# Attention queries and keys projected with tokens as columns, values for all heads at once, row sums of squares gathered through DRAM

## The chip, the core and the metric

The kernel runs on one core of one Trainium2 chip. The metric is the device time of one execution in microseconds, lower is better. The names of the profile are used throughout: PE is TensorE (matmuls), PEld its weight loads, DVE is VectorE, ACT is ScalarE, POOL is GpSimd, SP is SyncE, whose queue issues most DMAs. A bank is one 128 x 512 float32 tile of the accumulator memory that PE writes.

## What is computed

One decoder layer on 1024 tokens of width 1024, in float32: a normalised input goes through one input projection; half of its columns feed four heads of differential attention (this case), the other half a gated delta rule that runs chunk by chunk over the sequence (called the scan below); both go through one output projection and a squared-ReLU MLP. The part that the change touches:

```python
da_q = rms_norm(da_q.reshape(B, S, DA_HEADS, 2, DA_QK_DIM), q_norm_w[l])   # 4 heads x 2 maps x 64
da_k = rms_norm(da_k.reshape(B, S, DA_HEADS, 2, DA_QK_DIM), k_norm_w[l])
da_v = da_v.reshape(B, S, DA_HEADS, DA_V_DIM)                              # 4 heads x 128
...
s = jnp.einsum('bqhcd,bkhcd->bhcqk', qb, k) * scale       # causal, two maps per head
p = jax.nn.softmax(s, axis=-1)
a = p[:, :, 0] - lam * p[:, :, 1]
out = jnp.einsum('bhqk,bkhe->bqhe', a, v)
```

So each query and each key is divided by the root of the mean square of its own 64 numbers, and multiplied by a learned weight, before the products.

## The kernel before, in words

Every large product is made of three float32r matmuls (high part by high part, high by low, low by high), so a 128-deep slice of a product costs three matmuls. `hH` and `hL` hold the normalised input as high and low parts, features on partitions, tokens as columns.

The program has four stretches on PE. First the input norm, the z gate and the scan's own projections (`ps_z`, `ps_dn`; the latter, in `trn`, already has weights stationary and 512 tokens moving). Second the attention projections (`ps_qk`), with the scan (`ps_A`, `ps_o` of lines 1079 and 1095) and the attention of heads 0 and 1 (`ps_sc` scores, `ps_at` transposes of the exponentials, `ps_o` of line 1465) put between. Third the output projection (`ps_op`) with the attention of heads 2 and 3 between. Last the MLP (`X`, `Y`, `Z`).

From the second stretch on, the order of all engines is written by a planner, the class `Interleave`. Streams of PE work with priorities (the scan first, then attention, then `da_units`, then the output projection) yield small pieces; tasks stand for the work of ACT, DVE, POOL and SP, with assumed costs (`act`, `vec`, `powr`, `load`, `STORE`). The planner keeps its own clock and emits each engine's instructions in the order in which its model would start them. On the chip each engine then runs its own list in that order, and waits where an operand is not there.

`da_units` (line 1196) is the filler of the second stretch. It makes 48 units: for each of two head groups `g` the keys, the queries and the values, each for 8 blocks of 128 tokens. A unit has 24 matmuls into 256 columns of a bank: 128 tokens stationary (`hH`, `hL`), 256 weight columns moving. Two banks (`pj`) take turns. `normed` (line 1218) then empties a unit: for values ACT copies it and POOL stores it; for queries and keys ACT squares it (line 1235) and copies it (line 1238), DVE sums the squares (`sn`, line 1241), DVE and POOL make the inverse root (`rn`, lines 938 and 940), and DVE multiplies (line 1247). `da_turns` (line 1157) turns the result by two PE transposes (`ps_qkt`, lines 1163 and 1164) so that features come on partitions, ACT applies the learned weight (line 1172), and POOL stores it to `q_d` or `k_d`.

`head_loads` (line 1279) later loads a head's keys and splits them in high and low parts (`KS`), then loads its values (`vt`); `query_loads` loads a block of queries. `open_unit` in `scores` makes the scores of one block of 128 queries; for each map one DVE instruction adds the mask and finds the row maximum (line 1349), ACT takes the exponential with that maximum as bias (line 1342), `joined` combines the two maps, and `values` multiplies with `vt`.

Weights come in pieces of 128 x 512 through two buffers (`wraw`), are split by ACT (line 979) and DVE (line 981), and lie in two sets of buffers that take turns (`wH`, `wL`), so the weights of the next unit but one can be split only when a set is free.

Of the kernel before, what the change touches and what calls it, by code (L numbers as in the profile page):

```python
# [9 lines left out]
F32 = mybir.dt.float32  # L10
# [22 lines left out]
INVERSES = 500.0  # L33
# [16 lines left out]
class Interleave:  # L50
# [101 lines left out]

    def until(self, res):
        return self.held.get(self.first(res[0]) if isinstance(res, list) else res, 0.0)
# [46 lines left out]
def tile_hymba_layer(  # L201
    ctx: ExitStack,
    tc: tile.TileContext,
    x, x_cols, w1_cols, w_z, w_units, lambda_q1, lambda_k1, lambda_q2, lambda_k2, q_norm_w, k_norm_w,
# [50 lines left out]
    q_d = dram.tile([2, NT, P, 2 * P], F32, name="q_d")  # L255
    k_d = dram.tile([2, 2, P, SEQ], F32, name="k_d")
    v_d = dram.tile([2, 2, P, NT, P], F32, name="v_d")
# [425 lines left out]
    def dn_proj(kind):  # L683
        for pr in range(2):
            with tc.issue_after(x_last.ins) if kind == 1 and pr == 0 else ExitStack():
                w = load_unit(w_units[6 + 2 * kind + pr])
# [218 lines left out]
    ap = dctx.enter_context(tc.tile_pool(name="ap", bufs=1, **right))  # L905
    sdctx = ExitStack()
# [12 lines left out]
    def bank_tile(pool, res, name):  # L919
        return pool.tile([P, 512], F32, tag=f"{res[0]}{res[1]}", name=name)  # L920

    state = dict(scan=False, da=0, proj=False, attn=False, free=False, out=False, o1=0, o2=0, gates=0, begun=0, units=0,
                 turned=0, rows=0, started=0, popped=0, valued=0, first=False, op=0)
# [11 lines left out]
    def root(o, ss, scale, pool, tag, n):  # L935
        yield vec(n)
        t = pool.tile([P, n], F32, tag=tag, name=tag) if pool else laid(tag)
        V.tensor_scalar(t, ss, scale, EPS, ALU.mult, ALU.add)
        yield powr(n)
        G.tensor_tensor(o, t, neghalf[:, :n], ALU.pow)  # L940
# [206 lines left out]

    def x_loads():
        yield when(lambda: state["scan"])
        for tb in tiles:  # L1150
            yield load(5300.0)
            nc.sync.dma_start(accs[tb], x2[tb * P:(tb + 1) * P, :])
            yield flow.t + 6000.0

    late, accs, over = [], {}, set()

    def da_turns():
        for i in range(4 * NT):
            yield lambda: late[0][0].done if late and state["units"] >= 4 else None, None
            r = yield from flow.bank("px")  # L1160
            _, g, kind, tb, qn = late.pop(0)
            pt = bank_tile(px, r, "ps_qkt")
            T.transpose(pt[:, 0:P], qn[:, 0:P], ident)
            T.transpose(pt[:, P:2 * P], qn[:, P:2 * P], ident)
            flow.pe(2 * TR)
            state["rows"] -= 1

            def weighed(r=r, pt=pt, g=g, kind=kind, tb=tb):
                wv = qw if kind == 0 else kw
                yield "S", 370.0  # L1170
                qa = sd.tile([P, 256], F32, tag="qa", name="qa", bufs=4)
                S.activation(qa, pt[:, 0:256], AF.Copy, scale=wv)
                flow.leave(r)
                yield STORE
                if kind == 0:
                    nc.gpsimd.dma_start(q_d[g, tb], qa)
                else:
                    nc.gpsimd.dma_start(k_d[g, :, :, tb * P:(tb + 1) * P].rearrange("h p t -> p h t"),
                                        qa.rearrange("p (h t) -> p h t", h=2))
                yield None  # L1180
                state["turned"] += 1

            flow.task(1, weighed(), "sd")
# [7 lines left out]
    def group_done(g, last):  # L1191
        yield when(lambda: state["turned"] >= 2 * NT * (g + 1))
        yield last
        state["da"] = g + 1

    def da_units():
        n = 0
        for i, (g, kind) in enumerate(todo_da):
            job = jobs[i]
            state["begun"] = i  # L1200
            for j in range(NT):
                tb = NT - 1 - j if i == len(todo_da) - 1 else j
                sl = slice(tb * P, (tb + 1) * P)
# [1040 lines left out]
```

## Time and profile before

The profiled execution took 1221.5 us, of which the span (first to last instruction of the core) is 1219.7 us; the rest, 1.8 us, lies around it. Three runs without a profile took 1221.91 to 1222.18 us, median 1221.97, so the profiled execution stands 0.5 us below the median.

| | span | PE | DVE | ACT | POOL |
|---|---|---|---|---|---|
| busy us | 1219.7 | 1208.5 | 848.9 | 630.7 | 163.6 |
| instructions | | 6807 | 1642 | 1293 | 219 |

A busy PE is one that has some matmul under way; since matmuls overlap (each is shown for longer than the distance to the next one), the distance from start to start, seen in the timeline, tells what a matmul costs. The second stretch runs from 223.1 us (first `ps_qk`) to 452.7 us (first `ps_op`), the third to 601.7 us (first `X`).

### The profile page before, as it was taken

How to read it: one execution, taken by the hardware profiler on the slowest of the kernel's cores; microseconds unless marked ns; L12 is line 12 of the kernel's file. 1: busy time of each engine (PE TensorE's matmuls, PEld its weight loads, DVE VectorE, ACT ScalarE, POOL GpSimd, SP SyncE). 2: the span in 40 equal slices, each digit the busy share in tenths (PEclk: the TensorE clock that was granted, in tenths of full speed). 3: DMA queues.
4: the chain of work that ended last, by engine and by line, in shares of the span. 5: the costliest groups of instructions: out<-in, count | busy, mean ns of one | idle time of the engine just before them, and what ended most of it. 6: DMA issues, size and time to landing. Idle time of an engine off the chain costs nothing.

```text
span 1219.7 us, 18864 instructions
## 1 busy us (share of the span) xinstructions
PE 1208.5 (99%) x6807; PEld 1037.2 (85%) x6807; DVE 848.9 (70%) x1642; ACT 630.7 (52%) x1293; POOL 163.6 (13%) x219
## 2 busy tenths in 40 slices
PE   9999999999999999999999999999999999999998
PEld 8978888899999988888878888888888888888887
DVE  5879897646468876897797655566579754777543
ACT  6588643345356765586666544455554333333331
POOL 2423210044336331012100000000000000000000
PEclk9999999999999999999999999999999999999999
DMA  9334654445654564223438343453479555423301
GB/s 348 98 112 123 189 154 80 95 133 173 229 200 141 149 151 160 71 44 110 155 97 293 138 141 136 156 190 138 160 272 382 221 185 186 148 103 104 138 35 69
DMA packets 160837, 189.26 MB, mean 155 GB/s; under 512 B 61240, under 2 KB 116840, under 8 KB 160744
## 3 DMA queue, kind: packets, MB, share of 16 engines
q1 hardware_dynamic: 157144, 178.62, 45.0%
q0 software_dynamic: 3456, 9.44, 2.2%
q8 instruction: 53, 0.87, 0.3%
q14 instruction: 40, 0.33, 0.1%
q10 hardware_dynamic: 144, 0.00, 0.0%
HBM read 127.21 MB, written 60.82 MB: 154 GB/s over the span
## 4 chain that ended last, share of the span: by engine, by line
PE 92%; DVE 3%; ACT 1%; DMA 1%; issue 1%; SPq 0%; POOL 0%; POOLq 0%; ACTq 0%; DVEq 0%
PE X L1824 4%; PE X L1823 4%; PE X L1825 4%; PE X L2145 4%; PE X L2143 4%; PE X L2144 4%; PE ps_qk L1210 4%; PE ps_qk L1211 3%; PE ps_qk L1212 3%; PE ps_dn L279 3%; PE ps_dn L281 3%; PE ps_dn L280 3%; PE ps_o L1465 2%; PE ps_op L1609 2%; PE Y L1825 2%; PE ps_op L1611 2%
## 5 line engine op out<-in xcount | busy, mean ns | idle before, releaser
L1700 ACT CAST hH<-ur 128x1024 fp32r<-128x1024 f32 x56 | 58.9, 1051 | 173.3 <-PE Y L2144 89.8
L1701 DVE TENSOR_TENSOR hL<-ur,hH 128x1024 fp32r<-128x1024 f32 x56 | 68.4, 1223 | 80.7 <-ACT hH L1700 80.7
L1210 PE MATMUL ps_qk<-wH,hH 128*128 128x256 f32 x384 | 114.8, 299 | 1.2 <-DVE sn L1241 1.2
L1701 DVE TENSOR_TENSOR op<-raw,op 128x1024 fp32r<-128x1024 f32 x48 | 58.7, 1224 | 74.3 <-PE X L1824 40.4
L1211 PE MATMUL ps_qk<-wL,hH 128*128 128x256 f32 x384 | 108.8, 283 | 0.0
L1212 PE MATMUL ps_qk<-wH,hL 128*128 128x256 f32 x384 | 108.6, 283 | 0.0
L2143 PE MATMUL X<-hH 128*128 128x512 f32 x224 | 87.1, 389 | 0.0
L2144 PE MATMUL X<-hL,hH 128*128 128x512 f32 x224 | 87.1, 389 | 0.0
L2145 PE MATMUL X<-hH,hL 128*128 128x512 f32 x224 | 87.1, 389 | 0.0
L1210 PEld LDWEIGHTS ps_qk<-wH,hH 128*128 128x128 f32 x384 | 73.3, 191 | 4.0 <-DVE sn L1241 1.6
L279 PE MATMUL ps_dn<-hH,wH 128*128 128x512 f32 x192 | 76.0, 396 | 0.5 <-ACT cp L695 0.5
L280 PE MATMUL ps_dn<-hL,wH 128*128 128x512 f32 x192 | 75.5, 393 | 0.0
L281 PE MATMUL ps_dn<-hH,wL 128*128 128x512 f32 x192 | 75.3, 393 | 0.0
L1211 PEld LDWEIGHTS ps_qk<-wL,hH 128*128 128x128 f32 x384 | 73.4, 191 | 0.1
L1212 PEld LDWEIGHTS ps_qk<-wH,hL 128*128 128x128 f32 x384 | 73.2, 191 | 0.0
L1701 DVE TENSOR_TENSOR hL<-dw,hH 128x1024 fp32r<-128x1024 f32 x56 | 68.3, 1219 | 1.8 <-ACT hH L1700 1.6
L1700 ACT CAST op<-raw 128x1024 fp32r<-128x1024 f32 x48 | 50.5, 1052 | 34.8 <-PE Y L1825 19.9
L1700 ACT CAST hH<-dw 128x1024 fp32r<-128x1024 f32 x56 | 58.7, 1048 | 10.9 <-DMA dw<-in_w_down_dram 6.0
L699 DVE SCALAR_TENSOR_TENSOR cy<-cp,pv,cy 128x512 f32<-128x512 f32 x72 | 58.4, 813 | 5.9 <-ACT cy L697 5.0
L1342 ACT ACTIVATE pexp<-pexp,mx 128x128 f32<-128x128 f32 (+7 forms) x64 | 49.6, 776 | 10.3 <-DVE mx L1349 9.8
L1609 PE MATMUL ps_op<-wH,hH 128*128 128x512 f32 x128 | 54.4, 425 | 0.0
L1825 PE MATMUL Y<-hH,op 128*128 128x512 f32 x128 | 49.9, 390 | 0.5 <-DVE op L1974 0.5
(382 smaller groups left out, 3422.7 us busy)
## 6 DMA issues: line engine op xcount, KB each, us to landing
ur<-ud SPq DMA_DIRECT2D x28, 1024.0 KB, 4.8
raw<-in_w_up_dram SPq DMA_DIRECT2D x32, 512.0 KB, 3.8
dw<-in_w_down_dram SPq DMA_DIRECT2D x32, 512.0 KB, 6.6
wraw<-in_w_units_dram SPq DMA_DIRECT2D x48, 256.0 KB, 3.5
ud<-ua SPq DMA_DIRECT2D x16, 512.0 KB, 4.0
ud<-s SPq DMA_DIRECT2D x16, 512.0 KB, 2.7
pka<-park_d SPq DMA_DIRECT2D x32, 192.0 KB, 4.4
xt<-in_x_dram SPq DMA_DIRECT2D x8, 512.0 KB, 10.3
```

Of the source, the lines that this page charges most:

```text
L279: T.matmul(ps, lh(k), rh(k), start=(k == 0), stop=False)
L280: T.matmul(ps, lh(k), rl(k), start=False, stop=False)
L281: T.matmul(ps, ll(k), rh(k), start=False, stop=(k == n - 1))
L1210: T.matmul(ps[:, :256], hH[:, k, sl], wh[:, k, :], start=(k == 0), stop=False)
L1211: T.matmul(ps[:, :256], hH[:, k, sl], wl[:, k, :], start=False, stop=False)
L1212: T.matmul(ps[:, :256], hL[:, k, sl], wh[:, k, :], start=False, stop=(k == KB - 1))
L1700: S.copy(dst[0], src)
L1701: V.tensor_tensor(dst[1], src, dst[0].bitcast(F32), ALU.subtract)
L1825: T.matmul(ps, op[1][:, k, cs], h[0][:, k, :], start=False, stop=stop and k == 3, skip_group_check=True)
L2143: T.matmul(bank[t], v[0][:, j, sl], v[2][:, j], start=s0, stop=False, skip_group_check=True)
L2144: T.matmul(bank[t], v[0][:, j, sl], v[3][:, j], start=False, stop=False, skip_group_check=True)
L2145: T.matmul(bank[t], v[1][:, j, sl], v[2][:, j], start=False, stop=s1, skip_group_check=True)
```

## The change

What it does, part by part:

- **Queries and keys.** A unit is now one head (128 features) by 512 tokens: 24 matmuls 512 wide, 128 weight columns stationary, 512 columns of `hH` or `hL` moving. There are 4 units for each of four weight blocks, 16 in all in place of 32 (`STEPS`: keys of heads 0 and 1, their queries, the values of all heads, keys of heads 2 and 3, their queries). The result has features on partitions, so `da_turns` and its transposes are gone.
- **Values.** One step for all four heads: 128 tokens by 512 columns, 8 units of 24 matmuls, in pairs that share the weights' two halves.
- **Emptying a unit** (`squares`): ACT copies it with the learned weight into SBUF, POOL stores it unnormalised to `qk_d`; ACT squares the bank in place; DVE turns it in 32 x 32 blocks (STREAM_TRANSPOSE) and sums along rows, which leaves partial sums over 32 features.
- **Gathering the sums** (`chain`, once for each of 8 head-and-kind pairs): DVE turns the partial sums, POOL stores them to `ss_d`, SP loads them back in another layout (`L`, four loads for queries, two for keys), DVE adds the halves, DVE and POOL make the inverse root of 16 columns at once. For queries the negated root stays in SBUF (`negq`). For keys it goes through DRAM again (`rk_d`).
- **Where the roots are applied.** Keys: `head_loads` loads the root row broadcast to 64 partitions twice, the keys, multiplies them on DVE into a bank, and splits from there. Queries: not multiplied at all; the exponential takes `negq` as its scale, and a new small DVE instruction (128 x 2, line 1453) multiplies the maximum by the root to make the bias, before the two exponentials of a block.
- Head 0's values are loaded in four pieces of two token blocks. Gates of the planner change with the new units (`INVERSES`, `fits`), and `x` is loaded for the residual at a closer pace.

```diff
-INVERSES = 500.0
+INVERSES = 650.0
...
+def squares(kind, h, hf, r, ps, first):
...
+    a = sd.tile([P, 512], F32, tag="a", name="qk", bufs=3)
+    S.activation(a, ps, AF.Copy, scale=qw if kind == 0 else kw)
+    flow.task(1, stored_half(kind, h, hf, a), "sd")
+    S.activation(ps, ps, AF.Square)
+    V.transpose(tq, ps)
+    flow.leave(r)
+    V.tensor_reduce(part[0][:, 16 * hf:16 * hf + 16], tq.rearrange("p (b i) -> p b i", i=32), axis=AX.X, op=ALU.add)
+    if part[1] == 2:
+        flow.task(2, chain(kind, h), "att")
...
+def chain(kind, h):
+    V.transpose(pT, parts.pop((kind, h))[0])
+    nc.gpsimd.dma_start(ss_d[i].rearrange("(p t) -> p t", t=32), pT)
+    if kind == 0:
+        for ti in range(4):
+            nc.sync.dma_start(L[32 * ti:32 * ti + 32], ss_d[i].rearrange("(x i t) -> x i t", i=4, t=32)[:, ti])
+        V.transpose(Lt, L)
+        V.tensor_tensor(rs.rearrange("p (m b) -> p m b", m=2), lv[:, :, 0], lv[:, :, 1], ALU.add)
+    else:
...
+    yield from root(rr, rs, 1.0 / DQK, sr, "rt", 16, 2)
+    if kind == 0:
+        V.tensor_scalar(negq[h], rr, -1.0, None, ALU.mult)
+    else:
+        nc.gpsimd.dma_start(rk_d[h].rearrange("m (p t) -> (m p) t", t=16), rr)
...
-                    T.matmul(ps[:, :256], hH[:, k, sl], wh[:, k, :], start=(k == 0), stop=False)
-                    T.matmul(ps[:, :256], hH[:, k, sl], wl[:, k, :], start=False, stop=False)
-                    T.matmul(ps[:, :256], hL[:, k, sl], wh[:, k, :], start=False, stop=(k == KB - 1))
+                    T.matmul(ps, wh[:, k, cs], hH[:, k, sl], start=(k == 0), stop=False)
+                    T.matmul(ps, wh[:, k, cs], hL[:, k, sl], start=False, stop=False)
+                    T.matmul(ps, wl[:, k, cs], hH[:, k, sl], start=False, stop=(k == KB - 1))
...
     def head_loads(h, pool, gate, value_gate):
+        for m in range(2):
+            nc.sync.dma_start(rk[HF[m]], rk_d[h][m].partition_broadcast(64))
-        nc.sync.dma_start(raw, k_d[h // 2, h % 2])
+        nc.sync.dma_start(raw, qk_d[4 + h])
         for cs in (slice(0, 512), slice(512, SEQ)):
-            S.copy(KS[0][:, cs], raw[:, cs])
-            V.tensor_tensor(KS[1][:, cs], raw[:, cs], KS[0][:, cs].bitcast(F32), ALU.subtract)
+            V.tensor_tensor(ps, raw[:, cs], rk[:, cs], ALU.mult)
+            S.copy(KS[0][:, cs], ps)
+            V.tensor_tensor(KS[1][:, cs], ps, KS[0][:, cs].bitcast(F32), ALU.subtract)
...
-                S.activation(e, e, AF.Exp, scale=-1.0, bias=mx[:, npc - 1, m:m + 1], accum_out=ssum[:, m:m + 1])
+                S.activation(e, e, AF.Exp, scale=negq[h][:, 8 * m + tb:8 * m + tb + 1], bias=bi[:, m:m + 1],
+                             accum_out=ssum[:, m:m + 1])
...
+                    V.scalar_tensor_tensor(bi, mx[:, npc - 1], -1.0, negq[h][:, tb::8], ALU.mult, ALU.mult)
```

Line numbers from here on in the changed program are its own. How the order of the engines moves is shown at three places.

PE in the middle of the second stretch of the kernel before, where one transpose pair stands inside a unit of queries:

```order
L1210 MATMUL ps_qk<-wH_2937,hH 128x256
L1211 MATMUL ps_qk<-wL_2938,hH 128x256
L1212 MATMUL ps_qk<-wH_2937,hL 128x256
L1163 MATMUL ps_qkt<-ident,qn 128x128
L1164 MATMUL ps_qkt<-ident,qn 128x128
L1210 MATMUL ps_qk<-wH_2937,hH 128x256
```

PE in the same stretch of the changed program, where a step of the scan (line 1037) stands inside a unit:

```order
L1324 MATMUL ps_qk<-hH,wH_2958 128x512
L1325 MATMUL ps_qk<-hL,wH_2958 128x512
L1326 MATMUL ps_qk<-hH,wL_2959 128x512
L1037 MATMUL ps_A<-S_3144,pka 128x128
L1037 MATMUL ps_A<-S_3146,pka 128x128
L1037 MATMUL ps_A<-S_3158,pka 128x128
L1037 MATMUL ps_A<-S_3166,pka 128x128
L1324 MATMUL ps_qk<-hH,wH_2958 128x512
```

The matmuls of the projection are twice as wide and half as many, and the transposes between them are gone; the steps of the scan and of the attention still break into them.

DVE in the kernel before, where one unit of keys or queries is emptied (the sum of squares, the mean with its small constant, the product with the root), ahead of the scan's first states `S`:

```order
L1241 TENSOR_REDUCE sn<-ps_qk 128x4 [waits Activation_49]
L938 TENSOR_SCALAR rnt<-sn 128x4 [waits DVE_49]
L1247 TENSOR_TENSOR qn<-qn,rn 128x256 [waits PE_49,Pool_49]
L1017 COPY S_3256<-ps_A 128x128 [waits PE_49,Activation_49]
L1017 COPY S_3258<-ps_A 128x128
```

DVE in the changed program at the chain of head 0's queries. `Lt` turns the sums that came back from DRAM; `S` are the scan's states of its third chunk, `oc` the scan's output; `small_71` holds the negated roots:

```order
L1095 TENSOR_TENSOR oc<-ps_o_3396,eg 128x512 [waits PE_49]
L1200 STREAM_TRANSPOSE Lt<-L 128x32 [waits DMAHW5_49,DMAHW6_49,DMAHW1_49,DMAHW0_49]
L1203 TENSOR_TENSOR rs<-Lt 128x16 [waits DVE_49]
L948 TENSOR_SCALAR rt<-rs 128x16 [waits DVE_49]
L1113 TENSOR_TENSOR oc<-oc,ps_o_3415 128x512 [waits PE_49]
L1025 SCALAR_TENSOR_TENSOR S_3445<-S_3301,elast,ps_A 128x128 [waits PE_49,Activation_49]
L1025 SCALAR_TENSOR_TENSOR S_3448<-S_3311,elast,ps_A 128x128
L991 TENSOR_TENSOR wL_3443<-wraw,wH_3442 128x512 [waits PE_49,Activation_49]
L1025 SCALAR_TENSOR_TENSOR S_3466<-S_3316,elast,ps_A 128x128
L1215 TENSOR_SCALAR small_71<-rr 128x16 [waits Pool_49]
L1025 SCALAR_TENSOR_TENSOR S_3473<-S_3330,elast,ps_A 128x128
```

An instruction that waits for four DMAs now stands in front of the scan's states, and one that waits for POOL's root stands among them.

SP in the changed program ahead of that. `L` are the loads of the sums (they wait for the store to `ss_d`, a DMA of POOL's queue), `pka` and `pkb` the scan's operands of the next steps, `zgt` its gate:

```order
L1075 DMA pkb<-park_d 128x256 [waits DMAHW4_49,PE_49]
L1197 DMA L<-ss_d_97 32x32 [waits DMAHW5_49,DMASW2_49]
L1197 DMA L<-ss_d_97 32x32 [waits DMAHW6_49]
L1081 DMA zgt<-zg_d 128x512 [waits DMAHW7_49,DVE_49]
L1197 DMA L<-ss_d_97 32x32 [waits DMAHW0_49]
L1197 DMA L<-ss_d_97 32x32 [waits DMAHW1_49]
L1005 DMA pka<-park_d 128x384 [waits DMAHW2_49,PE_49]
```

The same place of the kernel before, between the loads for the same two chunks of the scan:

```order
L1065 DMA pkb<-park_d 128x256 [waits DMAHW2_49,PE_49]
L1065 DMA pkb<-park_d 128x256 [waits DMAHW3_49,PE_49]
L1071 DMA zgt<-zg_d 128x512 [waits DMAHW4_49,DVE_49]
L995 DMA pka<-park_d 128x384 [waits DMAHW5_49,PE_49]
L995 DMA pka<-park_d 128x384 [waits DMAHW6_49]
```

Loads of the sums now stand ahead of the scan's next operands on SP's queue.

340 lines of the change are left out of this document (207 added, 133 removed).

## The prediction

> **What bounds the kernel now.** I read the page's busy times first, then the stretches by window, then PE's waits, and at last the timeline, which alone shows what a matmul costs.
>
> ```profile
> PE 1208.5 (99%) x6807; PEld 1037.2 (85%) x6807; DVE 848.9 (70%) x1642; ACT 630.7 (52%) x1293; POOL 163.6 (13%) x219
> PEclk9999999999999999999999999999999999999999
> PE 92%; DVE 3%; ACT 1%; DMA 1%; issue 1%; SPq 0%; POOL 0%; POOLq 0%; ACTq 0%; DVEq 0%
> ...
> 0.00:223.10 223.10, 219.25 (x1231) 189.23 (x1232) 178.06 (x442) 138.06 (x382) 50.64 (x67) 1.00 0.53 157
> 223.10:452.70 229.60, 227.46 (x1964) 218.18 (x1963) 154.80 (x472) 124.07 (x358) 89.42 (x114) 1.00 0.55 161
> 452.70:601.70 149.00, 148.61 (x903) 123.07 (x902) 116.89 (x348) 94.78 (x266) 21.21 (x36) 1.00 0.33 98
> 601.70:1219.70 618.00, 613.20 (x2715) 506.70 (x2713) 399.12 (x383) 273.78 (x290) 2.37 (x2) 1.00 0.46 166
> ```
>
> PE is busy for 99% of the span at the full granted clock, and 92% of the chain that ended last is PE. The window rows give, after each window's length, the busy time of PE, PEld, DVE, ACT and POOL. In the second stretch, the one that is changed, PE is busy for 227.46 of 229.60 us and DVE for 154.80, or 67%. What PE waited for from 223 to 602 us:
>
> ```profile
> PE ps_qk L1210 <- DVE sn L1241: 1.2, 1, 1.2
> PE ps_o L1465 <- ACT at L1456: 0.7, 2, 0.4
> PE ps_p L840 <- ACT W L854: 0.2, 1, 0.2
> ```
>
> That is 2.1 us in all. So there is next to no wait to remove; a gain can only come from less PE work, and a loss from new waits.
>
> **The change, part by part.**
>
> *Matmuls.* The projections go from 1152 matmuls of 256 columns to 576 of 512, for the same multiplications. First and last row of an unbroken run of 256-wide ones; of a run of 512-wide ones whose weights are stationary, as they will be in the changed units; and of a short run in the third stretch (start and shown length in us):
>
> ```profile
> 331.17 0.28 PE L1212 MATMUL ps_qk<-wH,hL 128*128 128x256 f32 x1
> ...
> 335.13 0.28 PE L1212 MATMUL ps_qk<-wH,hL 128*128 128x256 f32 x1
> ...
> 109.65 0.39 PE L280 MATMUL ps_dn<-hL,wH 128*128 128x512 f32 x1
> ...
> 113.27 0.39 PE L281 MATMUL ps_dn<-hH,wL 128*128 128x512 f32 x1
> ...
> 559.98 0.39 PE L1610 MATMUL ps_op<-wL,hH 128*128 128x512 f32 x1
> ...
> 560.91 0.39 PE L1611 MATMUL ps_op<-wH,hL 128*128 128x512 f32 x1
> ```
>
> From 331.17 to 335.13 there are 33 steps, 0.120 us each. From 109.65 to 113.27 there are 16, 0.226 us each; from 559.98 to 560.91, between pieces of attention, 4 steps take 0.93 us, 0.2325 each. A matmul twice as wide thus takes 1.89 to 1.94 times as long. 1152 x 0.120 = 138.2 us. 576 x 0.226 = 130.2 us, 576 x 0.2325 = 133.9 us. The new units stand between pieces of scan and attention, some less torn than the third stretch, so I take 0.229: 131.9 us. The term is **-6.3 us, bounds -8.0 and -4.3**.
>
> The Trainium skill speaks against this term: "TensorE: Matmul & The Clock Gate", section Back-to-back issue gap, gives the gap of a warm matmul as its columns over 2.4 GHz plus about 2.5 ns. By that, 256 columns would cost 109.2 ns and 512 columns 215.8, and the halving would save 1152 x 109.2 - 576 x 215.8 = 1.5 us. The trace disagrees, with 120 and 226 ns: more is lost per matmul here than the Trainium skill says, and the rows decide.
>
> *Transposes.* One pair inside a unit:
>
> ```profile
> 370.75 0.28 PE L1212 MATMUL ps_qk<-wH,hL 128*128 128x256 f32 x1
> 370.87 0.27 PE L1163 MATMUL ps_qkt<-ident,qn 128*128 128x128 f32 x1
> 370.98 0.27 PE L1164 MATMUL ps_qkt<-ident,qn 128*128 128x128 f32 x1
> 371.00 0.36 PE L1210 MATMUL ps_qk<-wH,hH 128*128 128x256 f32 x1
> 371.20 0.28 PE L1211 MATMUL ps_qk<-wL,hH 128*128 128x256 f32 x1
> ...
> 223.10:452.70 229.60, 12.40 (x64) 7.63 (x64) 15.12 (x32) 1.00 0.55 161
> ```
>
> Without the pair, the matmul at 371.00 would start at 370.87 and the next one 0.12 us after it, not 0.20: the pair costs 0.13 + 0.08 = 0.21 us, and 32 pairs **-6.7 us**. The last row is the busy time of all 64 transposes, 12.40 us; it counts their ends, which lie under the next matmul, so it is the far bound. Near bound: where a pair stands beside another break (scan, scores), the 0.08 us stay, and 32 x 0.13 = 4.2 us go. The breaks for scan and attention remain in number.
>
> *DVE, ACT and POOL.* The groups by line (busy us, mean ns of one), DVE's from 200 to 620 us, POOL's of the whole span:
>
> ```profile
> L1247 DVE TENSOR_TENSOR qn<-qn,rn 128x256 f32<-128x256 f32 x32 | 13.5, 422 | 15.4 <-POOL rn L940 13.5 <-PE ps_qk L1212 1.9
> L1241 DVE TENSOR_REDUCE sn<-ps_qk 128x4 f32<-128x256 f32 x32 | 13.4, 418 | 5.6 <-ACT qn L1238 5.4
> L938 DVE TENSOR_SCALAR rnt<-sn 128x4 f32<-128x4 f32 x32 | 5.7, 177 | 1.4 <-POOL rn L940 0.9
> L1127 DVE STREAM_TRANSPOSE oc<-zgt 128x512 f32<-128x512 f32 x8 | 5.6, 699 | 0.0
> L1289 DVE TENSOR_TENSOR KS<-KS,KS 128x512 fp32r<-128x512 f32 x8 | 5.5, 683 | 0.0
> L1363 DVE SCALAR_TENSOR_TENSOR cf<-ssum,nlam,ri 128x1 f32<-128x1 f32 x32 | 6.9, 217 | 0.5
> L1015 DVE SCALAR_TENSOR_TENSOR S<-S,elast,ps_A 128x128 f32<-128x128 f32 x24 | 7.1, 344 | 3.0 <-PE ps_A L1047 2.8 <-ACT wH L979 0.3
> L940 POOL TENSOR_TENSOR rn<-rnt,neghalf 128x4 f32<-128x4 f32 x32 | 34.2, 1070 | 88.2 <-DVE rnt L938 86.7 <-DVE of L1119 0.9
> L940 POOL TENSOR_TENSOR of<-oft,neghalf 128x1 f32<-128x1 f32 (+1 forms) x40 | 27.3, 682 | 113.5 <-DVE oft L938 110.1 <-DVE nss L1641 3.0 <-DVE of L1489 0.3
> ```
>
> Gone from DVE: 32 x (0.422 + 0.418 + 0.177) = 32.5 us. Added: 32 transposes of 0.70; 32 sums of 512, which no row shows (at least the 0.418 of 256, at most twice that; I take 0.69, as other 512-wide operations); 8 products for the keys of 0.683; 32 biases of 0.217; 8 chains of some five operations of about 0.17. That is 22.4 + 22.1 + 5.5 + 6.9 + 6.8 = 63.7 us, net **+31 us on DVE**. DVE then has about 186 of 217 us in this stretch, 86%, which PE still covers, in the mean; I cost it at nothing. Without that cover every DVE microsecond is one of PE. ACT swaps four 256-wide operations for two 512-wide, near nothing. POOL's 32 roots of 4 columns become 8 of 16: (1.070 - 0.682) / 3 = 0.13 us per column, an estimate of 2.6 us each, 21 us in place of 34.
>
> *Waits.* Head 0's chain for queries is the sharpest place. In the order shown ahead, `Lt` waits for loads that wait for a store, with the scan's states behind it on DVE; late states hold `ps_A` on PE.
>
> ```profile
> v_d<-qn POOLq DMA_DIRECT2D x16, 128.0 KB, 3.2
> gb<-fsg_d SPq DMA_DIRECT2D x32, 16.0 KB, 1.7
> qa<-q_d SPq DMA_DIRECT2D x32, 64.0 KB, 2.7
> xt<-in_x_dram SPq DMA_DIRECT2D x8, 512.0 KB, 10.3
> ```
>
> Store 3.2 and load 1.7 to 2.7 make about 6 us. Between the transpose that feeds the store and `Lt` stand 24 other DVE operations: 8 of 512 columns (0.69), 14 of 128 (0.34) and two small ones (0.17), some 10.6 us, so the loads should be there 4 us early. The roots are nearer: `small_71` waits for a POOL root of 2.6 us that began 2.4 us of DVE work earlier, so a few tenths can be lost at each of four heads (2.4: one product of 0.68, three states of 0.344, one split of 0.69). The keys of head 0 have four DRAM steps, 6 + 2.6 + 6 plus some 6 us of engine work, about 21 us, and 67 us of PE work stands between their last unit and the first score. **+1 us for all new waits; bounds 0 and +30** (below).
>
> The Trainium skill has a rule against such loads: "DMA: Bandwidth & Descriptors", Specifications, wants pieces of at least 512 bytes. The row of `gb`, whose pieces are 128 bytes like the new `L`, shows 1.7 us for 16 KB, so here small pieces do not make a small load late.
>
> **Sum:** -6.3 - 6.7 + 1.0 = -12.0 us. Against the profiled execution (1221.5 us, 0.5 below the median of the runs) that is **1209.5 us**. The known terms alone give 1221.5 - 8.0 - 12.4 = 1201 and 1221.5 - 4.3 - 4.2 = 1213 at their bounds; the near end with some waits reaches 1220.
>
> **Rivals.**
>
> *The second half of the value weights comes late.* Its buffers are free only when the last unit of the first queries ends, and 24 matmuls of values and one scan step, about 6.4 us, later PE needs it. Two of its four pieces have landed by then, the others are loaded only when the first two are split.
>
> ```profile
> L981 DVE TENSOR_TENSOR wL<-wraw,wH 128x512 fp32r<-128x512 f32 x38 | 26.0, 685 | 14.5 <-ACT wH L979 14.2
> L979 ACT CAST wH<-wraw 128x512 fp32r<-128x512 f32 x43 | 26.3, 619 | 26.7 <-PE ps_qk L1212 10.6 <-DMA wraw<-in_w_units_dram 10.2 <-PE ps_op L1611 3.1
> wraw<-in_w_units_dram SPq DMA_DIRECT2D x48, 256.0 KB, 3.5
> ```
>
> Split 1.3, load 3.5, split 1.3: the third piece is ready after 6.1 us, and the order wants it after about 8.7. For it: 2.6 us of reserve is little with DVE at 86%. Against it: scan steps stand between the pieces. Price 3 to 8 us with similar places: about 1215.5.
>
> *The pitch is proportional to the width*, so that only the transposes are saved: 512 columns would cost 2 x 0.120 = 0.240 us, and the time is 1221.5 - 6.7 + 1 = 1215.8. This is the Trainium skill's formula above in kind, less its 1.5 us. Two runs of rows, 0.226 and 0.2325, speak against it.
>
> *Slower: the query chains hold the scan.* If store and load each take what the slowest row above shows, 10.3 us, the chain takes 20.6, DVE stands 10 us before `Lt`, the scan's states wait, and PE, which runs its list in order, with them; 4 query chains make +40, so 1221.5 - 13 + 40 = 1248. It turns the result where one chain stalls 13 / 4 = 3.3 us or more, that is where store and load take 14 us. For it: all else on SP's queue stands behind those loads. Against it: 10.3 us belongs to the start, where many loads run at once; of the loads of the second stretch the slowest kind has a median of 4.4 us.
>
> ```profile
> pka<-park_d SPq DMA_DIRECT2D x32, 192.0 KB, 4.4
> ```
>
> **How the numbers follow.** My case, PE work less 13 with about 1 us of waits: 0.70, within 1205 to 1213. More saved, towards 12.4 for the transposes: 0.06, 1203. Late weights: 0.11. Proportional pitch: 0.04. Slower: 0.09. The range from **1203 to 1220** holds the first four but a little. A measurement here can tell about 0.2%, 2.4 us, from no change: faster (under 1219.5) 0.87; same 0.05, the late weights at their worst; slower 0.08.
>
> **What would show it.** Right: `ps_qk` and `ps_v` start every 0.226 to 0.233 us, the second stretch is about 12 us shorter, the third and last keep their lengths, and PE's waits stay under 4 us. Wrong: a pitch of 0.240; PE waits on DVE `S` or `sr`, with DVE idle before `Lt`; waits on `wL` at the first `ps_v`. A DVE share over 95% in the second stretch would make DVE the bound and the prediction wrong.

## The result, and the profile after

Six runs of the changed kernel took 1216.02 to 1219.46 us, median 1217.33; six of the kernel before took 1220.2 to 1222.18, median 1221.91. The ratio is 0.9968, 95% interval 0.9955 to 0.9981: faster by 4.6 us, where 12 were forecast. The profiled execution (1219.46 us) is the longest of the six, 2.1 us above their median; a run of matmuls at half pace at 73 us, in code that the change doesn't touch, holds 1.6 of it. The granted clock of PE is 0.50 there, from 73.4 to 76.8 us; three of the six runs have a mean granted clock of 1.000 and so no such stretch.

Of the page after, the busy times and the chain that ended last (PE's share of that chain was 92% before):

```profile
PE 1200.3 (99%) x6167; PEld 998.8 (82%) x6167; DVE 850.7 (70%) x1650; ACT 618.7 (51%) x1221; POOL 142.9 (12%) x183
...
PE 85%; DMA 4%; DVE 4%; ACT 3%; issue 2%; SPq 1%; POOL 1%; POOLq 0%; DVEq 0%; ACTq 0%
```

The same four stretches (length, then busy time of PE, PEld, DVE, ACT, POOL):

```profile
0.00:224.70 224.70, 219.16 (x1231) 188.85 (x1232) 176.85 (x442) 138.16 (x382) 49.74 (x67) 0.99 0.52 156
224.70:447.30 222.60, 217.88 (x1327) 180.08 (x1326) 152.03 (x443) 108.32 (x285) 63.05 (x76) 1.00 0.60 175
447.30:599.50 152.20, 150.09 (x899) 123.03 (x898) 122.90 (x384) 98.72 (x267) 27.73 (x38) 1.00 0.34 98
599.50:1217.70 618.20, 613.15 (x2715) 506.86 (x2713) 398.88 (x383) 273.54 (x290) 2.37 (x2) 1.00 0.47 166
```

The second stretch lost 7.0 us of length (229.6 to 222.6), not 12, and the third gained 3.2 (149.0 to 152.2). PE stood 2.1 us of the second before, now 4.7. Its waits there and in the third:

```profile
PE ps_o L1568 <- DVE KS L1372: 2.0, 1, 2.0
...
PE ps_at L1548 <- DVE KS L1372: 1.5, 1, 1.5
PE ps_sc L1475 <- ACT qa L1400: 1.3, 1, 1.3
PE ps_A L1046 <- DMA pka<-park_d: 1.0, 3, 0.4
```

Busy time hides what a matmul costs, so I added up the distances from each matmul's start to the next one's, by the kind of the first. Where a distance is over 0.13 us longer than usual for its pair of kinds, the excess is put to "stalls". In us, from the traces of one execution each:

```
                          before     after   change   forecast
projections (ps_qk, ps_v)  145.72    138.66    -7.06    -6.3
their transposes             5.00      0       -5.00    -6.7
all other matmuls         1052.01   1053.59    +1.58     0
stalls                      11.02     19.25    +8.23    +1
sum                       1213.75   1211.50    -2.25   -12.0
```

By this count the work fell by 10.5 us and stalls took 8 back. The first two rows hardly depend on the count: 12.1 us less, where 13 were forecast. How the 9.8 us of the other two rows divide does depend on what is called usual (with other choices the stalls rose by 5 to 9 us); their sum does not. Stalls by place: 252 to 270 us (start of the scan) +2.3, 300 to 350 -1.4, 400 to 500 us (called the seam here, where the second stretch passes into the third) +6.0, of which 1.3 are half pace, the first 100 us, which the change does not touch, +1.2.

### The profile page after: what moved, and what is told of

Same layout as the page of the kernel before. It is cut to its first block, busy times and chain, and to the rows that moved or that the text cites. A ratio compares the mean times of both kernels' runs of the same rounds, so it can differ in the third digit from the quotient of the medians.

```text
span 1217.7 us, 17427 instructions
## 1 busy us (share of the span) xinstructions
PE 1200.3 (99%) x6167; PEld 998.8 (82%) x6167; DVE 850.7 (70%) x1650; ACT 618.7 (51%) x1221; POOL 142.9 (12%) x183
## 4 chain that ended last, share of the span: by engine, by line
PE 85%; DMA 4%; DVE 4%; ACT 3%; issue 2%; SPq 1%; POOL 1%; POOLq 0%; DVEq 0%; ACTq 0%
PE X L1926 4%; PE X L1925 4%; PE X L1927 4%; PE X L2253 4%; PE X L2251 4%; PE X L2252 4%; PE ps_dn L288 3%; PE ps_dn L290 3%; PE ps_dn L289 3%; PE Y L1927 2%; PE Y L1926 2%; PE Y L1925 2%; PE ps_o L1568 2%; PE ps_op L1712 2%; PE Y L2253 2%; PE Y L2251 2%
## 5 line engine op out<-in xcount | busy, mean ns | idle before, releaser
L1437 ACT ACTIVATE pexp<-pexp,mx,small 128x128 f32<-128x128 f32 (+7 forms) x64 | 55.1, 863 | 11.5 <-DVE mx L1453 11.5
L1324 PE MATMUL ps_qk<-hH,wH 128*128 128x512 f32 x128 | 52.6, 411 | 0.0
L1714 PE MATMUL ps_op<-wH,hL 128*128 128x512 f32 x128 | 50.6, 395 | 0.0
L1326 PE MATMUL ps_qk<-hH,wL 128*128 128x512 f32 x128 | 50.6, 395 | 0.0
L1325 PE MATMUL ps_qk<-hL,wH 128*128 128x512 f32 x128 | 50.4, 394 | 0.0
L1927 PE MATMUL Y<-hH,op 128*128 128x512 f32 x128 | 49.9, 390 | 0.5 <-DVE op L2082 0.5
L1713 PE MATMUL ps_op<-wL,hH 128*128 128x512 f32 x128 | 50.3, 393 | 0.0
L1925 PE MATMUL Y<-hH,op 128*128 128x512 f32 x128 | 49.9, 390 | 0.0
```

The costliest lines, as they stand in the source:

```text
L1925: T.matmul(ps, op[0][:, k, cs], h[0][:, k, :], start=start and k == 0, stop=False, skip_group_check=True)
L1927: T.matmul(ps, op[1][:, k, cs], h[0][:, k, :], start=False, stop=stop and k == 3, skip_group_check=True)
```

## The experiments

Each version was timed beside the kernel before on the same chip. A profile is one execution, and the executions of one kernel lie 2 to 7 us apart from the fastest to the slowest, so the place of a stall is read from the trace and its price from the median. The intervals below reach 1 to 2 us to either side, so two versions whose medians are within 2 us of each other are not told apart.

The theories have letters, also in the expectations: A, loads of `x` crowd the seam. B, the keys' products on DVE. C, PE's own work fell by less. D, too few matmuls left at the scan's start. E, the chains' loads hold SP's queue. F, the seam's traffic as a whole. H, the order was merely written anew. J, the chains' place in time.

All runs (the median of before was 1221.6 to 1222.4 in each set; "PE busy" is out of the 90 us from 390 to 480):

| run | median us | ratio, interval | projections | stalls | PE busy |
|---|---|---|---|---|---|
| before | 1221.91 | | 145.72 | 11.02 | 89.50 |
| changed | 1217.33 | 0.9968 (0.9955, 0.9981) | 138.66 | 19.25 | 85.02 |
| e1 | 1225.24 | 1.0031 (1.0020, 1.0042) | 138.97 | 25.41 | 84.88 |
| e2 | 1215.34 | 0.9957 (0.9944, 0.9971) | 139.09 | 14.71 | 87.79 |
| e3 | 1214.73 | 0.9948 (0.9936, 0.9960) | 137.88 | 15.18 | 90.00 |
| e4 | 1221.81 | 0.9999 (0.9990, 1.0007) | 145.74 | 13.90 | 85.41 |
| e5 | 1217.53 | 0.9965 (0.9952, 0.9978) | 141.31 | 13.88 | 85.01 |
| e6 | 1222.96 | 1.0009 (0.9997, 1.0020) | 137.10 | 21.37 | 84.09 |
| e7 | 1245.46 | 1.0192 (1.0176, 1.0207) | 136.59 | 44.50 | 82.21 |
| e8 | 1220.55 | 0.9990 (0.9981, 0.9999) | 139.92 | 18.90 | 85.19 |
| e9 | 1221.00 | 0.9996 (0.9987, 1.0006) | 138.61 | 19.70 | 88.30 |
| e10 | 1218.23 | 0.9972 (0.9961, 0.9983) | 138.77 | 19.56 | 85.95 |
| e11 | 1218.38 | 0.9974 (0.9963, 0.9985) | 138.80 | 16.80 | 87.19 |
| e12 | 1222.77 | 1.0008 (1.0000, 1.0017) | 138.34 | 20.59 | 82.98 |
| e13 | 1222.88 | 1.0005 (0.9996, 1.0013) | 145.47 | 11.74 | 88.05 |
| e14 | 1221.29 | 0.9993 (0.9985, 1.0002) | 145.72 | 11.00 | 89.63 |
| e15 | 1226.22 | 1.0039 (1.0025, 1.0053) | 141.49 | 23.57 | 84.02 |
| e16 | 1226.36 | 1.0037 (1.0023, 1.0050) | 141.62 | 23.17 | 84.34 |
| e17 | 1237.66 | 1.0134 (1.0116, 1.0152) | 137.42 | 36.91 | 83.33 |
| e18 | 1235.09 | 1.0110 (1.0092, 1.0129) | 137.19 | 33.72 | 84.05 |

### The work itself: e4

```diff
-T.matmul(ps, wh[:, k, cs], hH[:, k, sl], start=(k == 0), stop=False)
+for c in (0, 256):       # two halves; the other two products and ps_v likewise
+    T.matmul(ps[:, c:c + 256], wh[:, k, cs], hH[:, k, s2], start=(k == 0 and c == 0), stop=False)
```

> Each of the 576 projection matmuls of 512 columns is done as two of 256, for the same sums, with all else as in the changed kernel. By the prediction's rows: 1152 matmuls at 0.120 us against 576 at 0.229, +6.3 us (bounds 4.3 and 8.0), 1223.6 us, if PE's own work sets the time; +3 us or less where the new waits would hide part of it. By the proportional formula (0.240 us for 512 columns): no change, 1217 us.

The projections went back to 145.74 us, to 0.02 of before, so the width alone is worth 7.1 us of PE's work: 0.0123 us for each of 576 pairs. The time rose by 1221.81 - 1217.33 = 4.5 us. The rival of a pitch proportional to the width, by which nothing would change, falls. At the seam e4 stands as the changed kernel does (PE busy for 85.41 of 90 us), so the width of the matmuls does not make the waits there.

### The start of the scan: e4 and e5

Windows from 252 to 270 us (the second number is PE's busy time), of the kernel before:

```profile
252.00:270.00 18.00, 17.95 (x155) 17.67 (x153) 8.03 (x23) 8.27 (x21) 9.40 (x11) 1.00 0.46 145
```

Of the changed kernel:

```profile
252.00:270.00 18.00, 16.89 (x152) 14.36 (x151) 10.61 (x25) 5.99 (x14) 3.53 (x2) 1.00 0.30 96
```

Of e4:

```profile
252.00:270.00 18.00, 18.00 (x172) 17.41 (x169) 10.47 (x24) 6.20 (x14) 5.32 (x5) 1.00 0.52 154
```

Of e5:

```profile
252.00:270.00 18.00, 18.00 (x149) 16.34 (x149) 10.80 (x24) 5.61 (x13) 5.34 (x5) 1.00 0.57 177
```

The scan's first products need `pka`, which SP can load only when the inverses (`ps_h`) are done. Before, 72 projection matmuls of 256 columns (8.6 us) stood between the inverses and the first `ps_A`, over those loads. After, between two steps of the inverses stand 16 to 24 matmuls, each of twice the width: up to the last inverses 99 in all, where there were 96 narrow ones. They are used up there, the inverses end at 265 and not at 252 us, with the first `ps_A` between their last pieces, and nothing is left over the loads. With narrow matmuls (e4) the hole is gone. e5 narrows the first few only:

```diff
+step = 256 if state["units"] < 8 else 512
+for c in range(0, 512, step):    # the first four half units
```

> Only the first four half units of keys (96 of the 576 matmuls of 512 columns) are done 256 wide. Theory D (between the steps of the inverses the order puts about as many projection matmuls as before, each twice as long, so none is left between the inverses and the scan's first products, and the loads of pka stand bare): the waits of 262 to 266 us go (2.4 us less in the trace), 96 matmuls cost 96 x 0.012 = 1.1 us more, so 1 to 1.5 us less than the changed kernel, 1216 us. Rival (the loads of pka are late for reasons of their own, a queue or bandwidth): the waits stay, 1218 us.

The hole went, as D said, but the projections took 2.65 us more (141.31), where 1.1 were expected, and that is about what the hole had cost: the median is that of the changed kernel, where D had 1216. In e4, too, the 7.1 us of added work cost only 4.5, and the other 2.6 are near the 2.3 of the hole that is gone. So what makes the hole is shown; that a kernel without it is faster, no run shows by itself.

### The seam

What stands in one of its holes, from the chain of waits of the changed kernel (start, length, what):

```profile
433.05 5.73 DMA mt<-mixn_d
...
438.88 0.17 ACT hH L1631
...
439.70 0.59 ACT qk L1238
440.29 0.50 ACT ps_qk L1241
...
441.97 0.59 DVE hL L1633
442.56 0.59 DVE part L1250
...
443.77 0.66 DVE KS L1372
...
444.56 0.91 PE ps_o L1568 x6
```

ACT reaches `hH` before the mixed rows `mt` have landed; behind it in ACT's list stand the emptying of a unit, behind that in DVE's the sums and the keys' split, and what `ps_o` needs. Each engine is idle for a part of that time. SP had been held, too. The lines below show its longest wait in 380 to 480 us and what it issued afterwards; the queries issued at 415.13 landed after 6.31 us and gave the 1.3 us wait at 420.

```profile
SPq L1207 <- DMA ss_d<-pT: 10.5, 1, 10.5
```

```profile
407.95 1.27 SPq L1207 DMA_DIRECT2D L<-ss_d  x2
...
411.34 0.58 SPq L1393 DMA_DIRECT2D qa<-qk_d  x1
...
415.13 0.38 SPq L1393 DMA_DIRECT2D qa<-qk_d  x1
```

**e1**, the spacing of `x` as before:

```diff
-yield flow.t + 700.0
+yield flow.t + 6000.0
```

> Only the loads of x are spaced as in the kernel before (6.0 us of planned time between them in place of 0.7). Theory A (crowded loads: the eight 512 KB loads of x come close together at the end of the second stretch, delay the queries' and the mixed rows' loads on SP's queue, and PE waits for what hangs on them): 3 to 5 us less than the changed kernel, some 1213 us; PE's waits for qa and for ps_o in the window 415 to 447 us are under 1 us in all. Theory B (new DVE and ACT work at the seam, above all the keys' products, delays what PE waits for): within 1 us of the changed kernel, 1217 us, the same waits. Theory C (PE's own work became less by fewer than 13 us): also 1217 us.

7.9 us more than the changed kernel. A in this form falls: PE's waits are as long at the seam and go on behind it, and `qa` still took 4.1 us to land.

**e2 and e3** leave work out: e2 the rows of the roots and the keys' products, e3 the squares and the chains as well.

```diff
-nc.sync.dma_start(rk[HF[m]], rk_d[h][m].partition_broadcast(64))
-V.tensor_tensor(ps, raw[:, cs], rk[:, cs], ALU.mult)     # e2: split raw itself
-V.transpose(tq, ps)                                       # e3: also all from Square to chain
+V.tensor_scalar(negq[h], neghalf[:, :16], 2.0, None, ALU.mult)
```

> Leaves out the roots' broadcast loads (8 of 256 KB) and the 8 products of keys by their roots, so the keys are split as they were stored; the chains of the keys still run. Theory B: 3 to 5 us less than the changed kernel, some 1213 us, no wait of PE that ends with a DVE line of KS. Theory A: 1 us less at most, 1216.5 us, since the loads of x stay close together. Theory C: 1217 us.

> Leaves out the squares, their sums through DRAM, all roots of queries and keys and the keys' products; the exponential's scale is the constant -1. PE has the same matmuls as in the changed kernel. If PE's own work became 13 us less and waits took the rest back (theories A and B): 1209 to 1211 us, PE's waits in the second and third stretch under 4 us in all, by B more surely than by A. Theory C: 1214 us or more with PE's waits under 4 us.

From 390 to 480 us, the kernel before:

```profile
390.00:480.00 90.00, 89.50 (x680) 79.87 (x680) 69.07 (x218) 58.66 (x161) 30.09 (x45) 1.00 0.60 161
```

The changed kernel:

```profile
390.00:480.00 90.00, 85.02 (x457) 66.25 (x457) 71.73 (x215) 53.54 (x131) 30.16 (x35) 0.98 0.72 194
```

e2:

```profile
390.00:480.00 90.00, 87.79 (x504) 68.89 (x503) 74.38 (x236) 57.06 (x141) 31.68 (x37) 1.00 0.66 181
```

e3:

```profile
390.00:480.00 90.00, 90.00 (x538) 72.83 (x538) 70.45 (x223) 58.92 (x142) 15.87 (x28) 1.00 0.67 189
```

Without the roots PE does not stand at all at the seam, though DVE is as busy (70.45) as in the changed kernel (71.73). So it is not DVE's load but the waits within the lists. In time this is little: e2's 1215.34 lies between what B (1213) and the others (1216.5, 1217) expected and is not told from the changed kernel, and e3 is 2.6 us below it, where the intervals still touch. e3's time, 1214.73, is not the 1209 to 1211 of theories A and B: its trace has the hole of the scan's start still (5.5 us in 250 to 300 us, with the granted clock at 0.50 from 265.7 to 269.1) and 2.2 us at 547 us for late weights. C holds in part: stalls apart, PE's work is 10.5 us less than before's in the changed kernel and 12.7 in e3, not 13.

**e6**, the chains' loads on POOL's queue, and **e8**, that with e5's edit:

```diff
-yield load(2500.0)
-nc.sync.dma_start(L[...], ...)
+yield "G", 590.0, 2500.0
+nc.gpsimd.dma_start(L[...], ...)
```

> The small loads of the root chains are issued on POOL's queue, behind the store that they wait for, and not on SP's. Theory E (the chains' loads stand at the head of SP's queue until the store has landed, once for 10.5 us, and the loads of queries, mixed rows and keys pile up behind): SP no longer waits for the store of the squares, PE's wait for the queries at 420 us (1.4 us) and most of that of ps_o at 442 us (2.1 us) go, 2 to 4 us less than the changed kernel, 1214 us. Theory B (DVE's work of the keys' products delays them): at most 1 us less, 1216.5 us, and PE still waits at 442 and 471 us for what stands behind KS on DVE.

> The edits of the two runs before it together: first four half units 256 wide, chain loads on POOL's queue. If both theories D and E hold, the gains add: 3 to 5 us less than the changed kernel, 1213 us, and PE's stalls beyond its normal pitch are near those of the kernel before. If the order shifts and new waits come in place of the old ones: 1215 us or more.

5.6 us more than the changed kernel, and 3.2 with e5's edit. SP's 10.5 us and PE's wait for queries are gone, but PE waits 4.1 us for DVE's `acc`, in the chain behind a `KS` load that took 9.4 us and an `mt` for which ACT stood 8.2. And the wait for the store has moved into POOL's list (e6, from 425 to 470 us):

```profile
POOL L L1197 <- DMA ss_d<-pT: 6.8, 1, 6.8
```

So freeing SP's queue in this way gains nothing, and E is not borne out; what the time would be with no engine held was not run.

**e7 and e12** change only numbers by which the planner writes the order:

```diff
-return "V", 68.0 + 1.045 * n + extra
+return "V", 150.0 + 1.06 * n + extra          # e7
-yield load(3400.0)   # mt
+yield load(6000.0)                            # e12; queries 2800 -> 4500
```

> The program is the same, but the planner that writes the order counts a DVE operation at the length that the trace shows (150 ns + 1.06 ns a column in place of 68 + 1.045). If the order was written too tight because DVE's operations are priced too low (theory B's form in the planner): PE's waits of 400 to 480 us halve at least, 2 to 4 us less than the changed kernel, 1214 us. By theory E the price changes little: 1216 to 1219 us.

> The program is the same, but the planner counts on a landing of mt after 6.0 us (3.4 in the changed kernel) and of the queries after 4.5 (2.8), nearer to the 3.8 to 6.7 and 3.6 to 6.3 us seen at the seam. Theory F in the form of order (the late loads cost because ACT's and DVE's orders put their users too early): PE's stalls of 400 to 480 us halve, 2 to 4 us less than the changed kernel, 1214 us. If the loads are late by themselves and PE needs the data: 1217 us or more, the same waits at other places.

28 and 5.4 us more than the changed kernel. Truer prices did not give a better order.

**e9 to e11** take the traffic apart: e9 without `x`, e10 with the roots' rows but no product, e11 with the product but no rows.

```diff
-nc.sync.dma_start(accs[tb], x2[tb * P:(tb + 1) * P, :])
+G.memset(accs[tb], 0.0)                                   # e9
-V.tensor_tensor(ps, raw[:, cs], rk[:, cs], ALU.mult)      # e10: none, split raw
+V.tensor_tensor(ps, raw[:, cs], raw[:, cs], ALU.mult)     # e11, and no loads of rk_d
```

> Leaves out the eight loads of x (4 MB, from 397 us on); POOL writes zeros in their place, so the residual is missing from the sums. Theory F (between 390 and 480 us more is moved than before, 17.4 against 14.5 MB; loads land late, ACT and DVE stand in order behind the late mt and qa, and PE behind them): mt and qa land in the 2.7 and 2.8 us of the kernel before, PE's stalls of 400 to 480 us fall from 6.8 to under 3 us, 3 to 5 us less than the changed kernel, 1213 us. Theory B (DVE's own work of the keys' products): the stalls and the time stay, 1216 to 1218 us.

> Leaves out the 8 products of the keys; the roots' rows are still loaded (8 of 256 KB), so this is the run without both plus the loads alone. Theory B (the product on DVE): like the run without both, 1215.3 us, PE's stalls of 400 to 480 us about 3 us. Theory F (the loads): like the changed kernel, 1217.3 us, stalls of 5 us or more.

> Leaves out the loads of the roots' rows; the 8 products stay on DVE, with the keys multiplied by themselves. Theory F: like the run without both, 1215.3 us, with mt and qa landing earlier than in the changed kernel. Theory B: like the changed kernel, 1217.3 us, with PE's waits behind KS on DVE.

Landing times from 390 to 480 us (the last number, median us) of the mixed rows and the queries, in the kernel before:

```profile
mt<-mixn_d SPq DMA_DIRECT2D x32, 64.0 KB, 2.7
...
qa<-q_d SPq DMA_DIRECT2D x12, 64.0 KB, 2.8
```

In the changed kernel:

```profile
mt<-mixn_d SPq DMA_DIRECT2D x32, 64.0 KB, 3.8
...
qa<-qk_d SPq DMA_DIRECT2D x11, 64.0 KB, 3.6
```

In e9:

```profile
mt<-mixn_d SPq DMA_DIRECT2D x32, 64.0 KB, 2.8
...
qa<-qk_d SPq DMA_DIRECT2D x10, 64.0 KB, 2.9
```

Without the 4 MB of `x` both land as before, and PE stands 1.7 us at the seam in place of 5.0, as F said. PE's busy time rises by 3.3 us without `x`, 2.2 without the rows, 0.9 without the products and 2.8 without rows and products. But none of e9 to e11 is faster than the changed kernel: e9 lost 4.8 us at 573 us, where PE waits for DVE's `mx` in a list that was written otherwise, and had a granted clock of 0.50 from 575.8 to 582.6 us. e10 and e11 (1218.23 and 1218.38) are not told from the changed kernel, so taking out the products alone (B) or the rows alone (F) gains nothing that can be told. And in e3 the loads land as late (`mt` 3.7, `qa` 4.2) with no wait of PE: late loads alone do no harm. That they do it together with the chains' work in the same lists fits e2, e3 and e9, but no run shows it by itself.

**e13 and e14** edit only the planner's numbers in the kernel before: e13 with e12's landings, e14 with the changed kernel's spacing of `x`.

```diff
-yield load(3400.0)                  # e13: 6000.0; queries 2800.0 -> 4500.0
-yield flow.t + 6000.0               # e14: 700.0
```

> The kernel before with only the planner's numbers edited, as in the run with later landings planned: mt 6.0 in place of 3.4 us, queries 4.5 in place of 2.8. The program and its sizes are those of before. Theory H (PE's waits belong to the order as written; the order of before came out with almost none, and any edit writes another, which brings some 3 to 10 us of them): 3 to 6 us more than the kernel before, 1226 us, with PE's stalls over 15 us where before has 11.0. Theory F (the waits of the changed kernel come from its own added loads and work): within 1 us of before, stalls of 11 to 12 us.

> The kernel before with the loads of x at the changed kernel's spacing (0.7 us of planned time in place of 6.0). Theory H: 2 to 6 us more than before, and PE's new waits not all at the seam. Theory F: the closer loads make mt and qa land later, 1 to 4 us more, with the waits between 400 and 480 us behind mt or qa. If neither: as before, 1221.8 us.

0.9 us more and 0.7 less than the kernel before of their set (1222.03), where H had 2 to 6 more. These two new orders cost the old program nothing that can be told from no change, so the loss does not come with any new order; it needs something that the change adds. The order still counts in the changed program: there, edits of the planner's numbers alone (e1, e7, e12) cost 5 to 28 us, and an order of it without the waits is not ruled out. The window of e13, in which PE stands 2 us:

```profile
390.00:480.00 90.00, 88.05 (x682) 79.63 (x680) 68.19 (x218) 59.12 (x162) 31.19 (x45) 1.00 0.61 159
```

**e15 and e16**, e5's edit with `x` at 1.5 and 2.5 us of spacing (700.0 to 1500.0 and 2500.0):

> The changed kernel with the first four half units of keys 256 wide (no bare loads at the scan's start) and the loads of x at 1.5 us of planned spacing (0.7). Theory H: an order like any other, 1215 to 1222 us with stalls of 14 to 20 us. Theory F: fewer loads at once at the seam, 1 to 3 us less than with the first edit alone (1217.5), 1215.5 us.

> As the run before, with the loads of x at 2.5 us of planned spacing. Theory H: 1215 to 1222 us, not ordered by the spacing. Theory F: less than at 1.5 us, 1214 us.

8.7 and 8.8 us more than e5; F, which wanted less with wider spacing, is wrong on this, as in e1. The planner counts `x` as needed by the output projection's first sums, and with wider spacing those wait (2.6 us for `acc` in e15). That this is the whole price was not shown.

**e17 and e18** move two chains away from the seam:

```diff
-STEPS = ((1, 0), (0, 0), (2, 0), (1, 1), (0, 1))
+STEPS = ((1, 0), (0, 0), (1, 1), (2, 0), (0, 1))     # e17
+STEPS = ((1, 0), (1, 1), (0, 0), (2, 0), (0, 1))     # e18
```

> The changed kernel with its five steps in another order: the keys of heads 2 and 3 come before the values and not behind them, so that their two root chains and stores are over before the seam; the matmuls, chains, loads and products are the same in number. Theory J (PE's waits of 400 to 480 us need the chains' work and loads together with those of the attention and the mixed rows in that window): PE idle from 390 to 480 us falls from 5.0 to under 3 us, 2 to 4 us less than the changed kernel, 1214 us. Rival (the products and the roots' rows, which are loaded when a head begins, are what matters, or the attention starts later and loses its cover): 1217 us or more.

> As the run before, with all keys first, then the queries of heads 0 and 1, the values, the queries of heads 2 and 3. Theory J: as the run before, 1214 us, PE idle under 3 us from 390 to 480 us. Rival: the attention of head 0 starts still later, 1218 us or more.

20.3 and 17.8 us more than the changed kernel. J's remedy fails: with the values later, attention comes later, PE's work at the seam is no better covered, and from 480 to 630 us PE stands for over 10 us. Whether the chains' place alone mattered could not be told, since the values' place moved with it.

## Why the prediction was right in direction and wrong in size

*Matmuls, -6.3:* right, inside its bounds; -7.06, and e4 gives it back. The pitch after is 0.227 us (six steps from 440.85 to 442.21 in the timeline below). The formula of the Trainium skill ("TensorE: Matmul & The Clock Gate", Back-to-back issue gap), which that page gives for an isolated matmul and by which the halving would save 1.5 us, does not hold here: e4 and the changed kernel have 145.74 against 138.66.

*Transposes, -6.7:* mis-sized by 1.7. The 5.0 us of the transposes went, near the near bound of 4.2. The 0.08 us by which each pair broke the next step were not saved as a whole: e4's projections, with no pairs between them, take as long as before's, and pieces of the scan and of the attention break into them at more places.

*DVE, +31 at no cost:* the cost held, the count was wrong. There are 16 units with squares, not 32:

```profile
L1244 DVE STREAM_TRANSPOSE tq<-ps_qk 128x512 f32<-128x512 f32 x16 | 11.4, 713 | 11.9 <-ACT ps_qk L1241 11.7
...
L1250 DVE TENSOR_REDUCE part<-tq 128x16 f32<-128x512 f32 x16 | 10.9, 682 | 0.3
```

The durations, taken as 0.70 and 0.69, were right (0.713, 0.682). With 16 the net would have been +9; DVE's busy time of the whole page rose by 1.8 us. "PE still covers" was the wrong question: DVE's load never became the bound, and e3 shows the same load without a wait.

*Waits, +1, bounds 0 and +30:* **this step failed.** It measured +8.2 in the trace, of which 2.9 are half pace that three of the six runs do not have; by the medians (4.6 us gained, 12.1 us of work gone) some 7.5 came back. The step looked for waits in the chain's own place, head 0's `Lt`, with the loads there 4 us early. They were late instead: the stores to `ss_d` took 4.1 us and the loads of `L` 3.1 (medians), where 3.2 and 1.7 to 2.7 had been reckoned. DVE's wait from 224.7 to 297.2 us:

```profile
DVE Lt L1200 <- DMA L<-ss_d: 1.8, 1, 1.8
```

But no wait of PE on the scan's `S` or `sr` is among those listed, so PE was covered there. The scan's start was not looked at, and the order there showed it: matmuls that are twice as long, put by the same count between dependent steps, use up what covered the next loads. At the seam the step counted neither the added traffic (17.4 MB in place of 14.5 from 390 to 480 us, by the DMA view) nor that ACT and DVE, which run their lists in order, pass on each late load to work that did not need it.

*Rivals.* Late value weights: PE waited 0.3 us at `ps_v`, so no. Proportional pitch: its time, 1215.8, is nearest to the measured one, and its mechanism is the one that e4 refutes. Chains that hold the scan: no; but its remark that all on SP's queue stands behind those loads came true, for 10.5 us at a later chain; e6, without that wait of SP, was slower.

*Where the gain went:* in the trace, about 2.3 us went into the hole at the scan's start (gone in e4 and e5) and about 5 into the seam (gone in e3, and not brought by two new orders of the old program, e13 and e14). The rest is the half pace at 73 us and the scatter of one execution. In the medians less is confirmed: taking all of the roots' work out gave 2.6 us back (e3), and closing the hole by narrower matmuls none (e5). Which part of the change is enough to open the seam stays open: rows, products, chains and `x` each take a part in the trace, and no version with all the work was faster than the changed kernel (e5 equals it). The direction came out right by the terms of the work; that the waits, whose places the step had wrong, stayed below them was luck, since they reach +30 at their bound.

## What to carry to other kernels

When a change makes each piece of filler work twice as large at the same count, look for every place where dependent steps are spaced by pieces, and ask what the pieces behind them were covering. When a kernel is bound by one engine at 99%, saved work shortens it only as far as the others' in-order lists and their loads keep up: count the traffic that the change adds at the busiest place and follow one late load through each list. A mean load of 70% says nothing of that.

## What was not expected of the hardware

Around the hole at 442 us of the changed kernel:

```profile
440.85 0.39 PE L1326 MATMUL ps_qk<-hH,wL 128*128 128x512 f32 x1
...
442.21 0.39 PE L1326 MATMUL ps_qk<-hH,wL 128*128 128x512 f32 x1
444.56 0.91 PE L1568 MATMUL ps_o<-vt,at 128*128 128x128 f32 x6 [1.96 <-DVE KS L1372]
...
446.49 0.63 PE L1325 MATMUL ps_qk<-hL,wH 128*128 128x512 f32 x1
446.91 0.63 PE L1326 MATMUL ps_qk<-hH,wL 128*128 128x512 f32 x1
...
448.19 0.63 PE L1714 MATMUL ps_op<-wH,hL 128*128 128x512 f32 x1
448.62 0.48 PE L1712 MATMUL ps_op<-wH,hH 128*128 128x512 f32 x1
448.94 0.40 PE L1713 MATMUL ps_op<-wL,hH 128*128 128x512 f32 x1
```

After 2.35 us without a start, matmuls of 512 columns stand 0.427 us apart (446.49 to 448.19 in four steps, 0.425), not 0.227, until 448.6 us: a wait of 2.1 us cost 1.3 more. The granted clock is 0.50 from 445.4 to 448.8 us, which makes the 0.98 in the changed kernel's row for 390 to 480 us. The like came after 3.65 us in e1 and 4.34 us in e10, and after 1.73 us in e3; at 73 us of the changed kernel it came where no two starts in the 3 us ahead were more than 1.17 us apart. In e5 a hole of 2.49 us did not do it:

```profile
462.03 0.39 PE L1718 MATMUL ps_op<-wH,hL 128*128 128x512 f32 x1
464.52 0.47 PE L1716 MATMUL ps_op<-wH,hH 128*128 128x512 f32 x1 [2.10 <-DVE acc L1727]
464.83 0.40 PE L1717 MATMUL ps_op<-wL,hH 128*128 128x512 f32 x1
465.07 0.39 PE L1718 MATMUL ps_op<-wH,hL 128*128 128x512 f32 x1
```

So the length of the hole alone does not decide it. The Trainium skill ("TensorE: Matmul & The Clock Gate", What's actually happening) tells of a clock that halves after an idle window of about 3.4 us, and that the window runs freely. The half pace agrees, and so does its length, 3.4 us at 445.4 and at 73.4 us; holes of 2.35 us with it and 2.49 us without it show that here less than a whole window of idle can be enough, at some places.

The half pace also goes with the scatter between executions. Of the twelve runs of e6, the one with a mean granted clock of 1.000 took 1218.61 us, and the three with 0.996 took 1224.33 to 1225.92. In the changed kernel it does not decide: the three runs at 1.000 took 1216.02 to 1217.71 us, and one at 0.998 took 1217.16.

POOL's root of 16 columns took 2.97 us (mean of 8), where 2.6 was estimated from its columns.
